# Eight experts on one core: all stores behind the last load, the first two x loads on one queue, b1 behind the first weights

## The chip, the core and the metric

The kernel runs on one core of a Trainium2 chip. The metric is the device time of one execution in microseconds, as the median of several executions. Data moves between the chip's memory (DRAM) and the core's on-chip memory over 16 DMA engines that all queues of the core share. A transfer is issued by a queue's owner: POOL (GpSimd), ACT (ScalarE) or SP (SyncE).

## The reference

Eight experts, each with 256 rows of width 512 and an inner width of 2048. All inputs and the output are float32.

```python
"x":  (8, 256, 512)    "w1": (8, 512, 2048)    "w2": (8, 2048, 512)
"b1": (8, 2048)        "b2": (8, 512)

h = np.matmul(x, w1) + b1[:, np.newaxis, :]
h = np.maximum(h, 0)
return (np.matmul(h, w2) + b2[:, np.newaxis, :]).astype(np.float32)
```

## The kernel before

**What one expert needs.** Its w1 and its w2 (4 MB each in float32) are loaded by POOL's queue, which casts to float16 on the way, so that 2 MB each land on chip. x of experts 2 to 7 takes the same way (0.25 MB landing each). `transposes(e)` turns x with eight small TensorE products and one VectorE copy into `xT`. `first_product(e)` runs 16 groups of four products (w1 against `xT`); ScalarE adds b1 and applies the maximum while it moves each group into `hT`. In the middle of it, after the ninth group, TensorE does `transposes(e + 1)`. `second_product(e)` puts b2 into two accumulators and adds 32 products of `hT` with w2; `store` then copies one accumulator with VectorE and the other with ScalarE into an `out` tile (0.5 MB) that goes to DRAM.

**Order.** The main loop runs over steps s from 0 to 10. Step s does `first_product(s)` (while s < 8) and then `second_product(s - 3)` (`LAG` is 3). TensorE's instructions and POOL's DMAs keep the order of the program. The DMAs of POOL's queue come from the list `ring`: each entry has the step from which it may be issued, and the list is worked off from its head, so an entry also waits for those ahead of it. w1 and w2 have three buffers each, so the load of w1 of expert 3 waits for the first product of expert 0, and so on; w2 of expert 7 has buffers of its own and comes in five pieces of 4, 4, 4, 2 and 2 rows out of 16.

**Stores.** `flush(e)` issues the store of expert e on POOL's queue. In the kernel before, experts 0, 1 and 2 have their `flush` in `ring` among the loads (step 4 on); experts 3 to 6 (`LATE`) have it behind all loads. The store of expert 5 is cut by rows (`PARTS`): 25 partitions go by SP as soon as the tile is ready, 96 and 7 by POOL. Expert 7 is stored in two halves by SP and ACT (L148, L149) as soon as each is copied.

**Start.** x of experts 0 and 1 comes as float32, one by SP and one by ACT, in pieces of 2 KB (L173), into a tile of its own (`x32`), and VectorE casts it (L186). b1 comes by ACT's queue behind x of expert 1 (L174). POOL issues w1 of expert 0, then b2 (L176), then makes two identity matrices, then enters the main loop. TensorE's program begins with 64 small products that turn b1 (L191); VectorE copies the result (L199); then come `transposes(0)` and the first product of expert 0. The turned b1 and the turned x share one accumulator buffer, so `transposes(0)` waits for that copy.

The main loop, with what fills `ring`, stands in full below.

Of the kernel before, what the change touches and what calls it, by code (L numbers as in the profile page):

```python
# [11 lines left out]
def kernel(  # L12
# [9 lines left out]
    nc = tc.nc  # L22
    fp32 = mybir.dt.float32
    fp16 = mybir.dt.float16
    E, T, H = x.shape
    M = w1.shape[2]
    P = 128
    nTB = T // P
    nKC = H // P
    nJ = M // P  # L30
    LAG = 3
    LATE = (3, 4, 5, 6)

# [1 line left out]
    nXF32 = 2  # L37

    def ordered(ins):
        return tc.keep_in_program_order(ins)  # L40

    singles = ctx.enter_context(tc.tile_pool(name="singles", bufs=1))
# [2 lines left out]
    w2t_pool = ctx.enter_context(tc.tile_pool(name="w2t", bufs=1))  # L45
    x_pool = ctx.enter_context(tc.tile_pool(name="xp", bufs=4))
    xT_pool = ctx.enter_context(tc.tile_pool(name="xTp", bufs=2))
    hT_pool = ctx.enter_context(tc.tile_pool(name="hT", bufs=LAG + 2))
    out_pool = ctx.enter_context(tc.tile_pool(name="outp", bufs=5))
    psum_x = ctx.enter_context(tc.tile_pool(name="psum_x", bufs=1, space=bass.MemoryType.PSUM))  # L50
    psum_h = ctx.enter_context(tc.tile_pool(name="psum_h", bufs=3, space=bass.MemoryType.PSUM))
    psum_o = ctx.enter_context(tc.tile_pool(name="psum_o", bufs=2, space=bass.MemoryType.PSUM))
# [5 lines left out]
    b1_rows = singles.tile([E * 2, M // 2], fp32)  # L58
    b1T = singles.tile([P, nJ, E], fp32)

    x16 = [None] * E
# [3 lines left out]
    hT = [None] * E  # L65
# [8 lines left out]
    def load_w1(e):  # L74
        w1_sb[e] = w1_pool.tile([P, nKC, M], fp16, tag="w1", name="w1sb")
        ordered(nc.gpsimd.dma_start(  # L76
            out=w1_sb[e], in_=w1[e].rearrange("(p kc) m -> p kc m", kc=nKC)
        ))

    def load_w2(e):  # L80
        src = w2[e].rearrange("(p j) h -> p j h", j=nJ)
        w2_sb[e] = []
        t = w2_pool.tile([P, nJ, H], fp16, tag="w2", name="w2sb")
        step = nJ if e < E - 2 else nJ // 2
        for lo in range(0, nJ, step):
            ordered(nc.gpsimd.dma_start(out=t[:, lo : lo + step, :], in_=src[:, lo : lo + step, :]))  # L86
            w2_sb[e].append((lo, lo + step, t[:, lo : lo + step, :]))
# [80 lines left out]
                    ))  # L168
        store(e, po)

    x32 = singles.tile([P, nXF32, nTB, H], fp32)
    for e in range(nXF32):
        (nc.sync if e == 0 else nc.scalar).dma_start(out=x32[:, e], max_dma_last_dim=2048, in_=x[e].rearrange("(p tb) h -> p tb h", tb=nTB))  # L173
    nc.scalar.dma_start(out=b1_rows, in_=b1.rearrange("e (s i) -> (e s) i", s=2))  # L174
    load_w1(0)
    ordered(nc.gpsimd.dma_start(  # L176
        out=b2_sb,
        in_=b2.rearrange("e h -> (e h)").rearrange("(o f) -> o f", o=1),
    ))
    make_identity(nc, ident)  # L180
    make_identity(nc, ident16)
    nc.vector.memset(ones1, 1.0)

    for e in range(nXF32):
        x16[e] = x_pool.tile([P, nTB, H], fp16, tag="x16", name="x16")
        nc.vector.tensor_copy(out=x16[e], in_=x32[:, e])  # L186

    pb = psum_x.tile([P, nJ, E, 2], fp32, tag="psx", name="pb")
    for j in range(nJ):
        for s in range(2):  # L190
            ordered(nc.tensor.matmul(  # L191
                out=pb[s * 64 : (s + 1) * 64, j, :, :],
# [5 lines left out]
    for s in range(2):  # L198
        nc.vector.tensor_copy(  # L199
            out=b1T[s * 64 : (s + 1) * 64, :, :], in_=pb[s * 64 : (s + 1) * 64, :, :, s]  # L200
# [5 lines left out]
    ring = []  # L206
    for s in range(1, E + LAG - 1):
        if s < E:
            if s >= nXF32:
                ring.append((s - 2, load_x, (s,)))  # L210
            ring.append((s - 2, load_w1, (s,)))
        if s >= LAG:
            ring.append((s - 2, load_w2, (s - LAG,)))
        if s >= 2 * LAG and s - 2 * LAG not in LATE:
            ring.append((s - 2, flush, (s - 2 * LAG,)))
    for lo, hi in ((0, 4), (4, 8), (8, 12), (12, 14), (14, 16)):
        ring.append((0, load_w2_piece, (E - 1, lo, hi)))
    for e in LATE:
        ring.append((e + LAG + 1, flush, (e,)))
# [40 lines left out]
```

## Time and profile before

| | |
|---|---|
| median of 6 runs | 183.0 us (182.57 to 183.25) |
| the profiled execution | 182.7 us, of which the span is 180.9 us |
| TensorE busy | 138.3 us, 76% of the span |
| ScalarE busy | 62.6 us, 35% |
| VectorE, GpSimd busy | 13.2 us, 20.3 us |
| moved by DMA, counted where it lands | 40.58 MB, mean 224 GB/s |
| the same, by POOL's queue (q0) alone | 38.71 MB in 4928 packets |
| read from DRAM, written to it | 71.39 MB, 4.19 MB |
| granted TensorE clock, mean | 0.924 of full speed |

The profile is one execution. Its span runs from the first to the last instruction; the execution's own time is 1.8 us longer, and the median of the runs stands 0.3 us above that. The shares of busy time are means over the whole span; a packet's time on a DMA engine can overlap with its neighbour's, so the DMA shares can add up to slightly over 100%. Times within the span are given in us from its start.

### The profile page before, as it was taken

The numbers are of one execution on the slowest core, as the hardware profiler recorded it, in microseconds if no ns is written. First come the engines' busy times: TensorE is split into PE (matmuls) and PEld (weight loads), VectorE is DVE, ScalarE is ACT, GpSimd is POOL, SyncE is SP. The second block draws the span as 40 slices with busy tenths as digits, with TensorE's granted clock in tenths as the row PEclk, the third lists the DMA queues.
The fourth block names the chain that finished last, engine by engine and source line by source line (L and its number), as shares of the span: only waits on it lengthen the run. The fifth ranks groups of instructions, "written<-read, shape, count | busy, mean of one in ns | idle before, by whom it ended". The sixth has DMA issues, their size and how long they took to land.

```text
span 180.9 us, 2129 instructions
## 1 busy us (share of the span) xinstructions
PE 138.3 (76%) x912; PEld 95.7 (53%) x912; DVE 13.2 (7%) x21; ACT 62.6 (35%) x137; POOL 20.3 (11%) x44
## 2 busy tenths in 40 slices
PE   0555989489650999939990899918999994999991
PEld 0544879469550754936480664907549641334340
DVE  0320011001000101010100101001010010010101
ACT  0022779538560340825080250722409601010101
POOL 7200030300300010211010100200004201112100
PEclk9999999969995589999999589996999999699999
DMA  5989998998999899899989998999998999999995
GB/s 186 288 178 234 232 214 192 205 255 181 230 232 221 185 232 232 189 216 232 228 185 221 236 225 185 228 257 207 232 221 190 284 232 249 211 215 217 212 375 229
DMA packets 5831, 40.58 MB, mean 224 GB/s; under 512 B 670, under 2 KB 686, under 8 KB 3774
## 3 DMA queue, kind: packets, MB, share of 16 engines
q0 software_dynamic: 4928, 38.71, 97.4%
q1 hardware_dynamic: 446, 0.89, 1.4%
q10 hardware_dynamic: 448, 0.85, 1.3%
q8 instruction: 7, 0.11, 0.2%
q14 instruction: 2, 0.02, 0.0%
HBM read 71.39 MB, written 4.19 MB: 418 GB/s over the span
## 4 chain that ended last, share of the span: by engine, by line
DMA 59%; PE 24%; issue 9%; another core or an unknown queue 4%; POOL 2%; ACT 0%; POOLq 0%; ACTq 0%
DMA x<-in_x_dram 25%; DMA w2sb<-in_w_dram 21%; PE po L162 16%; DMA w1sb<-in_w_dram 13%; PE ph L114 6%; PE po L156 1%; PE psx L101 1%; POOL w2sb L86 1%; POOL w1sb L76 1%; ACT out L140 0%; POOL out_dram L135 0%; POOL b_sb L176 0%; POOL ident masks.py:199 0%; POOL ident masks.py:197 0%
## 5 line engine op out<-in xcount | busy, mean ns | idle before, releaser
L114 PE MATMUL ph<-xT,w1sb 128*128 128x256 f16 x512 | 68.2, 299 | 9.2 <-DMA w1sb<-in_w_dram 9.2
L121 ACT ACTIVATE hT<-ph,b1T 128x256 f16<-128x256 f32 x128 | 57.0, 473 | 43.6 <-PE ph L114 43.3
L114 PEld LDWEIGHTS <-w1sb 128*128 128x128 f16 x512 | 61.5, 149 | 15.3 <-DMA w1sb<-in_w_dram 10.2
L162 PE MATMUL po<-w2sb,hT 128*128 128x512 f16 x224 | 51.2, 388 | 2.4 <-DMA w2sb<-in_w_dram 2.4
L162 PEld LDWEIGHTS <-hT 128*128 128x128 f16 x256 | 24.9, 100 | 35.3 <-issue 8.1
L140 ACT COPY out<-po 128x512 f32<-128x512 f32 x8 | 4.7, 590 | 60.4 <-PE po L162 60.4
L101 PE MATMUL psx<-ident,x 128*128 128x128 f16 x64 | 6.6, 265 | 20.4 <-DMA x<-in_x_dram 19.8
L101 PEld LDWEIGHTS <-x 128*128 128x128 f16 x64 | 5.3, 128 | 21.5 <-DMA x<-in_x_dram 20.7
L107 DVE COPY xT<-psx 128x1024 f16<-128x1024 f16 x8 | 5.5, 691 | 82.2 <-PE psx L101 82.2
L76 POOL DMA_DIRECT2D w1sb<-in_w_dram x8 | 4.5, 558 | 60.1 <-PE ph L114 59.3
L139 DVE COPY out<-po 128x512 f32<-128x512 f32 x8 | 5.5, 692 | 73.0 <-PE po L162 73.0
L86 POOL DMA_DIRECT2D w2sb<-in_w_dram x8 | 4.3, 536 | 48.6 <-PE po L162 48.6
L191 PE MATMUL pb<-ident,b_rows 16*64 16x16 f32 x64 | 3.7, 265 | 6.6 <-DMA b_rows<-in_b_dram 6.6
L191 PEld LDWEIGHTS pb<-ident,b_rows 16*64 16x64 f32 x64 | 3.6, 198 | 6.5 <-issue 6.5
L162 PE MATMUL po<-w,hT 128*128 128x512 f16 x32 | 7.1, 379 | 0.0
L135 POOL DMA_DIRECT2D out_dram<-out x8 | 4.3, 534 | 22.5 <-DMA w2sb<-in_w_dram 12.2
L121 ACT ACT_TABLE_LOAD x1 | 1.3, 1283 | 11.0 <-DVE b1T L199 11.0
L156 PE MATMUL po<-b_sb,ones 1*128 1x512 f16 x16 | 4.8, 379 | 0.0
L92 POOL DMA_DIRECT2D w<-in_w_dram x5 | 2.7, 538 | 14.3 <-DMA w2sb<-in_w_dram 13.5
L70 POOL DMA_DIRECT2D x<-in_x_dram x6 | 3.3, 551 | 4.8 <-DMA w2sb<-in_w_dram 4.2
L156 PEld LDWEIGHTS <-ones 1*128 1x128 f16 x16 | 0.9, 92 | 2.1 <-issue 2.1
L186 DVE CAST x<-x 128x1024 f16<-128x1024 f32 x2 | 1.4, 694 | 4.4 <-DMA x<-in_x_dram 4.3
(9 smaller groups left out, 2.6 us busy)
## 6 DMA issues: line engine op xcount, KB each, us to landing
w1sb<-in_w_dram POOLq DMA_DIRECT2D x8, 2048.0 KB, 33.6
w2sb<-in_w_dram POOLq DMA_DIRECT2D x6, 2048.0 KB, 45.3
out_dram<-out POOLq DMA_DIRECT2D x6, 512.0 KB, 29.7
w2sb<-in_w_dram POOLq DMA_DIRECT2D x2, 1024.0 KB, 25.4
x<-in_x_dram POOLq DMA_DIRECT2D x6, 256.0 KB, 38.9
w<-in_w_dram POOLq DMA_DIRECT2D x3, 512.0 KB, 29.5
x<-in_x_dram ACTq DMA_DIRECT2D x1, 512.0 KB, 5.3
x<-in_x_dram SPq DMA_DIRECT2D x1, 512.0 KB, 4.5
```

What stands on the lines that cost most here:

```text
L76: ordered(nc.gpsimd.dma_start(out=w1_sb[e], in_=w1[e].rearrange("(p kc) m -> p kc m", kc=nKC)))
L86: ordered(nc.gpsimd.dma_start(out=t[:, lo : lo + step, :], in_=src[:, lo : lo + step, :]))
L101: ordered(nc.tensor.transpose(out=pt[:, kc, tb * P : (tb + 1) * P], in_=x16[e][:, tb, :].rearrange("p (q kc) -> p q kc", kc=nKC)[:, :, kc] ...
L107: nc.vector.tensor_copy(out=xT[e], in_=pt)
L114: ordered(nc.tensor.matmul(out=ph, lhsT=w1_sb[e][:, kc, :].rearrange("p (q j) -> p q j", j=nJ)[:, :, j], rhs=xT[e][:, kc, :], start=(kc == 0),
L121: nc.scalar.activation(out=hT[e][:, j, :], in_=ph, func=mybir.ActivationFunctionType.Relu, bias=b1T[:, j, e : e + 1], scale=1.0,)
L135: ordered(nc.gpsimd.dma_start(out=dst[p0:p1], in_=src[p0:p1]))
L139: nc.vector.tensor_copy(out=out_sb[:, 0, :], in_=po[0])
L140: nc.scalar.copy(out=out_sb[:, 1, :], in_=po[1])
L156: ordered(nc.tensor.matmul(out=t, lhsT=ones1, rhs=b2_sb[0:1, e * H : (e + 1) * H], start=True, stop=False,))
L162: ordered(nc.tensor.matmul(out=po[tb], lhsT=hT[e][:, j, tb * P : (tb + 1) * P], rhs=t[:, j - lo, :], start=False, stop=(j == nJ - 1),))
L191: ordered(nc.tensor.matmul(out=pb[s * 64 : (s + 1) * 64, j, :, :], lhsT=b1_rows.rearrange("r (q j) -> r q j", j=nJ)[:, :, j], rhs=ident[0 ...
```

## The change

Five things change.

- `LATE` becomes all of experts 0 to 6: their stores are issued behind the last load. The `out` pool has eight buffers where it had five; `hT` has four where it had five.
- x of experts 0 and 1 goes by SP alone, in rows of 4 KB, into two buffers of the `out` pool in place of a tile of its own.
- b1 is loaded by POOL's queue, behind w1 of expert 0 and b2.
- w2 of expert 5 is loaded in two halves, as that of expert 6 was already.
- w2 of expert 7 comes in three pieces of 8, 4 and 4 rows.

```diff
-    LATE = (3, 4, 5, 6)
+    LATE = range(E - 1)
...
-    hT_pool = ctx.enter_context(tc.tile_pool(name="hT", bufs=LAG + 2))
-    out_pool = ctx.enter_context(tc.tile_pool(name="outp", bufs=5))
+    hT_pool = ctx.enter_context(tc.tile_pool(name="hT", bufs=LAG + 1))
+    out_pool = ctx.enter_context(tc.tile_pool(name="outp", bufs=E))
...
-        step = nJ if e < E - 2 else nJ // 2
+        step = nJ if e < E - 3 else nJ // 2
...
-    x32 = singles.tile([P, nXF32, nTB, H], fp32)
+    x32 = []
     for e in range(nXF32):
-        (nc.sync if e == 0 else nc.scalar).dma_start(out=x32[:, e], max_dma_last_dim=2048, in_=x[e].rearrange("(p tb) h -> p tb h", tb=nTB))
-    nc.scalar.dma_start(out=b1_rows, in_=b1.rearrange("e (s i) -> (e s) i", s=2))
+        x32.append(out_pool.tile([P, nTB, H], fp32, tag="out", name="x32"))
+        nc.sync.dma_start(out=x32[e], in_=x[e].rearrange("(p tb) h -> p tb h", tb=nTB))
     load_w1(0)
     ordered(nc.gpsimd.dma_start(
         out=b2_sb,
         in_=b2.rearrange("e h -> (e h)").rearrange("(o f) -> o f", o=1),
     ))
+    ordered(nc.gpsimd.dma_start(out=b1_rows, in_=b1.rearrange("e (s i) -> (e s) i", s=2)))
...
-        nc.vector.tensor_copy(out=x16[e], in_=x32[:, e])
+        nc.vector.tensor_copy(out=x16[e], in_=x32[e])
...
-        if s >= 2 * LAG and s - 2 * LAG not in LATE:
-            ring.append((s - 2, flush, (s - 2 * LAG,)))
-    for lo, hi in ((0, 4), (4, 8), (8, 12), (12, 14), (14, 16)):
+    for lo, hi in ((0, 8), (8, 12), (12, 16)):
         ring.append((0, load_w2_piece, (E - 1, lo, hi)))
     for e in LATE:
         ring.append((e + LAG + 1, flush, (e,)))
```

## The prediction

> **What bounds the kernel now.** I looked first for the resource that is never idle. On the page, the busy share of the 16 DMA engines over 40 slices and the split by queue say:
>
> ```profile
> DMA  5989998998999899899989998999998999999995
> ...
> q0 software_dynamic: 4928, 38.71, 97.4%
> q1 hardware_dynamic: 446, 0.89, 1.4%
> q10 hardware_dynamic: 448, 0.85, 1.3%
> ```
>
> From the second slice to the last but one nothing falls below 80%, and POOL's queue (q0) fills nearly all of it. The chain that ended last agrees: DMA holds 59% of it, TensorE 24%. So I ask of each edit what it adds to or takes from the work of the DMA engines, and only then what it does to TensorE.
>
> Next, the waits, for what TensorE and POOL lose:
>
> ```profile
> PE psx L101 <- DMA x<-in_x_dram: 19.8, 4, 6.7
> PE ph L114 <- DMA w1sb<-in_w_dram: 9.2, 4, 3.6
> PE pb L191 <- DMA b_rows<-in_b_dram: 6.6, 1, 6.6
> PE po L162 <- DMA w2sb<-in_w_dram: 2.4, 1, 2.4
> POOL x L70 <- DMA w2sb<-in_w_dram: 4.2, 1, 4.2
> ```
>
> TensorE waits for data. POOL's last row is another thing: x of expert 7 is POOL's 19th DMA, and it is issued when the 11th has landed; the other waits of this sort have the same distance, so at most eight of POOL's DMAs are under way.
>
> Then the timeline, for start and end:
>
> ```profile
> 1.27 0.49 ACTq L174 DMA_DIRECT2D b_rows<-in_b_dram  x1
> 6.56 3.71 PE L191 MATMUL pb<-ident,b_rows 16*64 16x16 f32 x64 [6.56 <-DMA b_rows<-in_b_dram]
> 12.04 0.69 DVE L107 COPY xT<-psx 128x1024 f16<-128x1024 f16 x1 [1.14 <-PE psx L101]
> 15.56 6.40 PE L114 MATMUL ph<-xT,w1sb 128*128 128x256 f16 x36 [3.55 <-DMA w1sb<-in_w_dram]
> 25.77 0.53 POOL L76 DMA_DIRECT2D w1sb<-in_w_dram  x1 [20.31 <-PE ph L114]
> ...
> 153.06 8.75 PE L162 MATMUL po<-w2sb,hT 128*128 128x512 f16 x32 [2.42 <-DMA w2sb<-in_w_dram]
> 169.82 7.08 PE L162 MATMUL po<-w,hT 128*128 128x512 f16 x32
> 170.32 0.55 POOL L135 DMA_DIRECT2D out_dram<-out  x1 [3.08 <-ACT out L140]
> 177.60 0.37 ACTq L149 DMA_DIRECT2D out_dram<-out  x1
> ```
>
> TensorE ends at 176.9, and expert 7's stores follow. The trace's packet records show the other racer: POOL's queue ends on the 16 engines between 176.7 and 178.25; expert 7's 16 packets per engine (2 KB, 84 to 88 ns each) run from 178.16 to 179.6. On the slowest engines the two join without a gap. TensorE's chain and the DMA work end together, so taking time from TensorE alone brings nothing.
>
> **Part by part.** The trace records when the last engine reports each transfer. Differences of neighbouring reports are what a transfer costs in a full queue: a whole w1 or w2 9.7 us, a half 4.79 and 4.87 (w2 of expert 6), a 4-row piece 2.50, 2.42, 2.46, a 2-row piece 1.24, 1.32, an x 1.24.
>
> *Stores of experts 0 to 2.* Among loads they cost 1.31, 1.31 and 1.27; those of experts 3 and 4, among stores, 1.26 and 1.24. Seven stores have to be moved either way, 3.6 MB of them by POOL. Moving three saves 3.89 - 3 x 1.25 = 0.1 at most; I take -0.1, bounds -0.15 and 0. The loads do come earlier: w2 of expert 5 (whole at 153.0) by two stores, 2.5; the last piece, now at 172.6, by three. What they gain is given back as stores behind them.
>
> *w2 of expert 7.* Now 166.44 - 163.94 for the first piece, then 2.42, 2.46, 1.24, 1.32: 9.94. After: 4.87 + 2 x 2.46 = 9.79, so -0.15.
>
> *w2 of expert 5 in halves.* Expert 6's halves cost 4.79 + 4.87 = 9.66; expert 5's whole cost 153.01 - 143.35 = 9.66. So 0, at worst +0.1. The Trainium skill ("DMA: Bandwidth & Descriptors", Anatomy of one DMA — SWDGE (gpsimd) path) fits a GpSimd DMA with a fixed 2.0 us plus its bytes; an estimate by it would put +2.0 on this split and -4.0 on the two pieces fewer. The halves above show no fixed part while the queue is full.
>
> *x of experts 0 and 1, and b1.* Now 32 packets of 2 KB per engine, then b1's one of 4 KB (159 to 180 ns), fill the engines from about 2.2 to 5.2, and w1 of expert 0 starts on each engine within a few ns of b1's end (5.13 to 5.44). After: 16 packets of 4 KB; the nearest row is b1's own, 0.16, so 16 x 0.16 = 2.6 against 32 x 0.084 = 2.7. Without b1 (0.16) w1 can start 0.3 earlier, if it is ready: POOL issued it at 1.26, and it cannot be told how long before 5.13 it was. b1 is paid behind it: +0.16. So between -0.15 and +0.16; I take 0, the middle, since neither end is nearer. SP issues both x in turn (0.43 each, so the second from 1.2); the first x's 8 packets per engine last until about 3.5, and the second is there by then.
>
> *b1 late.* It lands behind w1 of expert 0 and b2 (reports up to 15.68) at about 15.9 instead of 6.43. From its landing to the end of xT's copy, 6.56 to 12.73, are 6.2 us; so the first product starts at 22.1 instead of 15.56. That is 6.5 us off TensorE, and it is covered: the first product takes 9.9 (15.56 to 25.47, at partly half clock) or 7.7 (that of expert 1), so w1 of expert 3 is issued at 30.1 to 32.3 instead of 25.77. The queue has w1 of expert 2 and x of expert 3 until 36.7 on its fastest engine. From issue to first packet POOL needs at most 3.87 (w1 of expert 0, 1.26 to 5.13), so an issue up to 32.8 leaves no gap. Later loads have more: w1 of expert 4 follows at 38 to 40, its turn in the queue is at 57. TensorE catches up at the wait for x of expert 4 (6.75 idle before 59.02). The Trainium skill (same page, Latency and other measured facts) gives a first byte of 0.6 us to SP's and ACT's queues and 1 us to GpSimd's; an estimate by it would charge b1 only 0.4. The row charges the place in the queue.
>
> *Waits and buffers.* hT with four buffers: the one that step s writes was last read by the second product of s - 4, just ahead in TensorE's order; nothing. `out` with eight: x32's two slots come free at the casts (6.8). Eight DMAs under way: the store of expert 6 then waits for the last piece (about 169.9), is issued by 170.9, while the stores ahead fill the queue to 175; no gap.
>
> *TensorE's end.* x of expert 7 comes 1.25 earlier, w2 of expert 5's halves by 145.3 and 150.2, so the 2.4 us wait and the cold start behind it go: second products of experts 5 and 6 end at about 156 and 164, that of expert 7, held by its first piece (164.8), near 172. Its stores go out at 173 in place of 177.6 and mix with POOL's. What is late next is POOL's store queue: slowest engine 178.25 + 1.3 for expert 7's packets = 179.55, as now, and then the same 0.9 to 1.3 us to the span's end.
>
> The sum: -0.1 - 0.15 + 0 + 0 = -0.25, bounds -0.4 and +0.1. Where TensorE's chain was sometimes the later racer, its 5 us of slack add a little: I allow down to -0.6. Span 180.65, with the 1.8 around it 182.45; the median stood 0.3 above this profile's time: 182.7.
>
> **The rivals.** A difference of over 0.2% (0.37 us) is about what a measurement of this kernel can tell from no change.
>
> *Faster, by the tail.* If the median of now is set by TensorE's chain ending late in most runs (the profile's 182.7 is below the median 183.0) and w1 of expert 0 also starts 0.3 earlier, -0.8: 182.2. For it: the two racers are within 0.2 us. Against: the profiled run shows the slowest engines without a gap. That all of TensorE's 4.7 us is won is excluded by the seven stores behind the last load: 7 x 1.25 = 8.7 from 169.9.
>
> *Slower, by a dry queue.* The late b1 decides if w1 of expert 3 is issued after 32.8; each us beyond is a us lost. If the first product runs at half clock from end to end, 64 x 0.178 + 0.9 = 12.3, the issue comes at 34.7 and costs up to 1.9; with half of the 3.87 allowed for issue, nothing. I price it +0.9: 183.9. Against: the clock rose after 4.7 us of work in the run of before, and here b1's products lie just ahead.
>
> *Slower, by one engine.* The end is the slowest engine's. The trace shows seven instruction fetches of 0.9 us each, spread over six engines; if they fall on an engine that is last, +0.5: 183.5.
>
> *No move.* The order of the queue changes nothing at either end: 183.0.
>
> **How the numbers follow.** The forecast has 0.62; its spread of -0.6 to +0.1 puts 0.27 of that beyond -0.37, 0.33 within it, 0.02 above. Faster by the tail 0.15, dry queue 0.10, one engine 0.08, no move 0.05. Faster 0.27 + 0.15 = 0.42; same 0.33 + 0.05 = 0.38; slower 0.02 + 0.10 + 0.08 = 0.20. The range leaves out half of the dry queue and the far end of the tail: 181.9 to 183.5.
>
> **What would show it.** TensorE's first product begins near 22 and w1 of expert 3 is issued at 30 to 32, with the DMA share still at 9 in slices 7 to 9. The wait of L162 for w2sb is gone or under 1 us. The last piece lands near 170, TensorE ends near 172, and the last slices hold stores at about 375 GB/s (slice 39 of now). The forecast is wrong if the DMA share falls below 8 in any slice between, or if the stores behind the loads cost clearly more or less than 1.25 us each.

## The result, and the profile after

| | before | changed kernel |
|---|---|---|
| median | 182.88 us (39 runs, 182.54 to 183.42) | 183.64 us (17 runs, 183.43 to 184.48) |
| ratio | | 1.0048, 95% interval 1.0039 to 1.0057 |
| profiled execution | 182.7 us | 183.55 us |
| its span | 180.9 us | 181.8 us |

The change makes the kernel slower by 0.76 us, and the profiled span is longer by 0.87. Page, by slices and by queue:

```profile
DMA  5998999899999999999999999999998999999992
GB/s 213 249 231 189 231 231 216 179 239 231 211 195 231 231 206 198 209 253 202 202 231 231 202 202 231 202 220 213 231 231 182 218 209 224 207 230 214 398 401 109
...
q0 software_dynamic: 4816, 38.77, 96.8%
q1 hardware_dynamic: 462, 1.41, 2.1%
q10 hardware_dynamic: 144, 0.26, 0.4%
```

The DMA engines are as full as before, and slices 38 and 39, at 398 and 401 GB/s, are the stores behind the last load; but the last slice is at 2, where it was at 5: the engines have less to do just before the span ends. The waits of TensorE in the changed kernel:

```profile
PE psx L101 <- DMA x<-in_x_dram: 17.6, 4, 6.8
PE pb L192 <- DMA b_rows<-in_b_dram: 16.0, 1, 16.0
...
PE ph L114 <- DMA w1sb<-in_w_dram: 1.4, 1, 1.4
...
PE po L162 <- DMA w<-in_w_dram: 0.6, 1, 0.6
```

TensorE waits 16 us for b1 instead of 6.6, and only 1.4 and 0.6 us for w1 and w2 (9.2 and 2.4 before). The timeline at the start, and at the end:

```profile
15.99 3.71 PE L192 MATMUL pb<-ident,b_rows 16*64 16x16 f32 x64 [15.99 <-DMA b_rows<-in_b_dram]
...
22.21 5.88 PE L114 MATMUL ph<-xT,w1sb 128*128 128x256 f16 x36 [0.78 <-DVE xT L107]
...
31.91 0.53 POOL L76 DMA_DIRECT2D w1sb<-in_w_dram  x1 [25.69 <-PE ph L114]
```

```profile
164.47 7.07 PE L162 MATMUL po<-w,hT 128*128 128x512 f16 x32 [0.63 <-DMA w<-in_w_dram]
...
169.96 0.55 POOL L135 DMA_DIRECT2D out_dram<-out  x1 [2.27 <-DMA w<-in_w_dram]
...
171.44 0.36 SPq L148 DMA_DIRECT2D out_dram<-out  x1
...
172.19 0.38 ACTq L149 DMA_DIRECT2D out_dram<-out  x1
```

The first product starts at 22.21, w1 of expert 3 is issued at 31.91, TensorE ends at 171.5 in place of 176.9, and expert 7's two stores are issued 5.8 and 5.4 us earlier than before (177.60 for the one by ACT; the one by SP is the line below, from before). So far all is as forecast.

```profile
177.28 0.35 SPq L148 DMA_DIRECT2D out_dram<-out  x1
```

The end is not. The trace's reports of landing (last of 16 engines) say what came last:

| | before | changed kernel |
|---|---|---|
| last piece of w2 of expert 7 | 173.88 | 169.38 |
| POOL's last DMA, the store of expert 6 | 178.59 | 179.47 |
| SP's half of expert 7 | 179.35 | 178.11 |
| ACT's half of expert 7 | 179.99 | 179.64 |

The DMA engines finish 0.35 us earlier (179.64 against 179.99), and yet the span ends 0.87 later. What lies between can be read from the instructions of the program's end (line L255 in the kernel before, L254 in the changed one): a DRAIN on each engine (in the kernel before those of TensorE and VectorE end at 176.95 and 177.30, just behind their last work), and then a barrier that GpSimd collects. Each row gives shortest, median and longest duration in ns and the first and last start. First before, then the changed kernel:

```profile
L255 POOLq DRAIN  x3: 46/107/9813, 170.3 to 180.6; - x3
L255 SPq DRAIN  x3: 7/7/7, 180.1 to 180.4; - x3
```

```profile
L254 POOLq DRAIN  x3: 46/102/11053, 169.9 to 181.5; - x3
L254 SPq DRAIN  x3: 7/7/7, 179.8 to 181.2; - x3
```

POOL's first DRAIN starts as it issues its last DMA and is the longest of its row: 170.29 + 9.81 = 180.11 before, 169.94 + 11.05 = 180.99 now. SP's DRAIN, which follows when SP has seen every queue's reports, signals at 180.13 before and at 179.90 now. Before, the two came within 0.03 us of each other. Now SP is done 1.1 us before POOL. And POOL's drain ends 1.52 us after the last report of POOL's own DMAs in both: 180.11 - 178.59 and 180.99 - 179.47. From there to the span's end are 0.79 us in both.

Why POOL's queue ends later is seen in the times from issue to landing of the last store of POOL and of the two of expert 7 (512 and 256 KB each), before:

```profile
out_dram<-out POOLq DMA_DIRECT2D x1, 512.0 KB, 8.3
```

```profile
out_dram<-out SPq DMA_DIRECT2D x1, 256.0 KB, 2.1
out_dram<-out ACTq DMA_DIRECT2D x1, 256.0 KB, 2.4
```

and in the changed kernel:

```profile
out_dram<-out POOLq DMA_DIRECT2D x1, 512.0 KB, 9.5
```

```profile
out_dram<-out SPq DMA_DIRECT2D x1, 256.0 KB, 6.7
out_dram<-out ACTq DMA_DIRECT2D x1, 256.0 KB, 7.4
```

Issued early, the stores of SP and ACT mix with POOL's: they take 6.7 and 7.4 us in place of 2.1 and 2.4. The packet records show the order: their first packet starts at 175.42, 4.0 us after its issue, with 167 data packets of POOL (0.68 MB) still to start, and 255 of their 256 packets start before POOL's last data packet ends. Before, 19 did. POOL's last DMA takes 1.2 us more (9.5 against 8.3). Counted another way: the last piece of w2 lands 4.50 earlier, and three more stores behind it cost 3.8, so POOL's last report would have come at 177.9 if expert 7 had stayed behind it; it came 1.6 later. The 0.5 MB of expert 7 would be 1.25 at the price of the other stores; the rest is not accounted for.

### The profile page after: what moved, and what is told of

The parts are those of the page before. It is cut to its first block, busy times and chain, and to the rows that moved or that the text cites. A ratio compares the mean times of both kernels' runs of the same rounds, so it can differ in the third digit from the quotient of the medians.

```text
span 181.8 us, 2121 instructions
## 1 busy us (share of the span) xinstructions
PE 134.5 (74%) x912; PEld 94.2 (52%) x912; DVE 13.2 (7%) x21; ACT 62.5 (34%) x137; POOL 20.5 (11%) x44
## 4 chain that ended last, share of the span: by engine, by line
DMA 64%; PE 26%; POOL 2%; issue 1%; DVE 1%; ACT 0%; POOLq 0%
DMA x<-in_x_dram 40%; DMA w<-in_w_dram 16%; PE po L162 12%; PE ph L114 10%; DMA b_rows<-in_b_dram 7%; PE pb L192 2%; PE psx L101 2%; POOL w2sb L86 1%; POOL w1sb L76 1%; PE po L156 1%; DVE xT L107 0%; DVE b1T L200 0%; ACT out L140 0%; POOL b_sb L176 0%; POOLq L243 0%
## 5 line engine op out<-in xcount | busy, mean ns | idle before, releaser
L114 PE MATMUL ph<-xT,w1sb 128*128 128x256 f16 x512 | 66.8, 297 | 2.1 <-DMA w1sb<-in_w_dram 1.4
L121 ACT ACTIVATE hT<-ph,b1T 128x256 f16<-128x256 f32 x128 | 56.9, 473 | 32.3 <-PE ph L114 32.2
L162 PE MATMUL po<-w2sb,hT 128*128 128x512 f16 x224 | 49.6, 379 | 0.0
L162 PEld LDWEIGHTS <-hT 128*128 128x128 f16 x256 | 24.4, 98 | 32.4 <-issue 4.0
L101 PE MATMUL psx<-ident,x 128*128 128x128 f16 x64 | 5.8, 243 | 18.3 <-DMA x<-in_x_dram 17.6
L101 PEld LDWEIGHTS <-x 128*128 128x128 f16 x64 | 4.7, 122 | 19.4 <-DMA x<-in_x_dram 18.6
L86 POOL DMA_DIRECT2D w2sb<-in_w_dram x9 | 4.8, 535 | 53.7 <-PE po L162 53.7
L92 POOL DMA_DIRECT2D w<-in_w_dram x3 | 1.6, 557 | 0.0
## 6 DMA issues: line engine op xcount, KB each, us to landing
w<-in_w_dram POOLq DMA_DIRECT2D x2, 512.0 KB, 32.3
```

Of the source, the lines that this page charges most:

```text
L101: ordered(nc.tensor.transpose(out=pt[:, kc, tb * P : (tb + 1) * P], in_=x16[e][:, tb, :].rearrange("p (q kc) -> p q kc", kc=nKC)[:, :, kc] ...
L114: ordered(nc.tensor.matmul(out=ph, lhsT=w1_sb[e][:, kc, :].rearrange("p (q j) -> p q j", j=nJ)[:, :, j], rhs=xT[e][:, kc, :], start=(kc == 0),
L121: nc.scalar.activation(out=hT[e][:, j, :], in_=ph, func=mybir.ActivationFunctionType.Relu, bias=b1T[:, j, e : e + 1], scale=1.0,)
L162: ordered(nc.tensor.matmul(out=po[tb], lhsT=hT[e][:, j, tb * P : (tb + 1) * P], rhs=t[:, j - lo, :], start=False, stop=(j == nJ - 1),))
```

## The experiments

The theory that came from this, the tail theory, is written in the expectations below: the span ends 0.79 us after the later of two times, POOL's last report + 1.5, and the other queues' last report + 0.14. Its constants are from the two profiles above. Its rivals: the work theory (only the amount and order of DMA work count) and the late b1. The kernel before was timed again beside each group of runs, with medians from 182.78 to 182.91; the changed kernel was not, so differences from its 183.64 can be off by some 0.1 us.

**The disputed cost by itself.** The kernel before, with one line changed:

```diff
-            nc.scalar.dma_start(out=dst[:, 1, :], in_=out_sb[:, 1, :])
+            nc.gpsimd.dma_start(out=dst[:, 1, :], in_=out_sb[:, 1, :])
```

> The kernel before, with the second half of expert 7's store issued by POOL in place of ACT; the same bytes at the same point. Tail theory (the program cannot end before POOL's drain, and that ends 1.52 us after the last of POOL's DMAs has reported; 0.79 us later the span ends): POOL's last DMA is now reported near 180.2 instead of 178.59, so the drain ends near 181.7 and the span at 182.5, 1.6 us more than before: about 184.5. Work theory (only the DMA engines' work and its order count): the same packets by another queue, 0 to +0.3 us.

Measured: 184.44 us against 182.78, ratio 1.0088 (1.0069 to 1.0107).

```profile
L255 POOLq DRAIN  x3: 46/98/3901, 178.0 to 182.4; - x3
L255 SPq DRAIN  x3: 7/7/7, 180.8 to 182.2; - x3
```

POOL's last report is at 180.37, its drain ends at 178.02 + 3.90 = 181.93, 1.56 later; SP signals at 180.86 and then waits for it. The data landed only 0.4 later than in the kernel before, the span is 1.8 longer. The rest is the drain, and the work theory's 0.3 is out.

**Stores alone.** The kernel before with `LATE = range(E - 1)`, four buffers of hT and seven of out.

> The kernel before with the stores of experts 0 to 6 all behind the last load (hT four buffers, out seven) and nothing else of the change. Tail theory: TensorE ends near 172, expert 7's stores mix with POOL's, POOL's queue reports last near 179.5 to 179.8, the span is 181.8 to 182.1: the whole loss, +0.8 to +1.2 us on before. Theory of the late b1 or of x on one queue: those are not in this kernel, so 0 to -0.2 us.

Measured: 182.96 against 182.78, ratio 1.0015 (1.0000 to 1.0031). The tail theory's number, +0.8 to +1.2, was wrong, since I had taken TensorE's end from the whole change. With w2 of expert 5 in one piece TensorE still waits for it, 2.1 us, and its 32 products take 8.65 us, where those of expert 7 take 7.08:

```profile
150.05 8.65 PE L162 MATMUL po<-w2sb,hT 128*128 128x512 f16 x32 [2.09 <-DMA w2sb<-in_w_dram]
...
174.17 0.35 SPq L148 DMA_DIRECT2D out_dram<-out  x1
174.48 0.38 ACTq L149 DMA_DIRECT2D out_dram<-out  x1
```

Expert 7 is stored at 174.2 and 174.5, not at 171.4 and 172.2, and less of it goes ahead of POOL: 93 of its 256 packets start before POOL's last data packet ends, only 17 of them more than 1 us before. POOL's last report is at 178.25, the others' at 179.50, and the profiled span is 180.56 where the theory's rule gives 180.55 from these reports. In this profile late stores alone are not the loss; they have to meet an early end of TensorE. But the profiled execution, 182.32, has the lowest of the twelve times; four of them are 183.5 to 183.7, as long as the changed kernel, and no profile shows what happened there.

**b1 by ACT again**, all else of the change kept.

> The changed kernel with b1 on ACT's queue again, so that TensorE's first product starts near 15.5 instead of 22. Tail theory: nothing that sets the end moves, within 0.2 us of the changed kernel (183.6). Late-b1 theory: the loss comes back, 182.7 to 182.9.

Measured: 183.94, ratio to before 1.0062 (1.0046 to 1.0078). That is 0.3 above the changed kernel, a little more than the 0.2 allowed, and away from the 182.7 to 182.9 of the late b1. The late b1 is out: with b1 early, the loss is all there. POOL's last report is at 179.78, the drain's end at 181.26, the span 182.04.

**A step made later.** In the changed kernel, the copies of expert 7 are held until an earlier store has landed, by a write into that store's tile. The first try (`HELD` is 4, and `outs[e]` is the tile of expert e):

```diff
...
+        if e == E - 1:
+            nc.vector.memset(outs[HELD][:, 0, 0:1], 0.0)
+            nc.scalar.copy(out=outs[HELD][:, 1, 0:1], in_=b1T[:, 0, 0:1])
...
```

> The changed kernel, with the copies and so the stores of expert 7 held back until the store of expert 4 has landed (one more memset and one more copy, each of one column, write into that store's tile first). Nothing is made shorter and one step is made later. Tail theory: POOL's queue reports last near 178.3 (179.47 less 1.2 to 1.3 of packets that no longer go ahead), drain at 179.8; the other queues report last near 179.6 to 179.8; span 180.6 to 180.9, 1.0 us less than the changed kernel and about as before: 182.6 to 182.9. Work theory: a later store can only end later, 183.6 to 184.3.

Measured: 192.06, ratio 1.0496 (1.0469 to 1.0523). This says nothing on the order of the stores: the two held instructions were placed ahead of the copies of experts 5 and 6, and TensorE found no free accumulator. The waits show it, the two held instructions (L143, L144) and TensorE behind ScalarE's copy:

```profile
ACT out L144 <- DMA out_dram<-out: 28.5, 1, 28.5
...
DVE out L143 <- DMA out_dram<-out: 22.6, 1, 22.6
...
PE po L162 <- ACT out L146: 12.5, 1, 12.5
```

Expert 7's product ended at 186.1. The second try keeps all copies in program order.

> As the run before it (the changed kernel with the copies of expert 7 held until the store of expert 4 has landed), with the copies of all experts kept in program order, so that only expert 7 is held; in the run before, those of experts 5 and 6 stood behind the held one too and TensorE lost 13 us. Tail theory: POOL's queue reports last at 178.2 to 178.5, drain 1.52 later, the other queues last at 179.6 to 179.9, span 180.6 to 180.9: 1.0 us less than the changed kernel. Work theory: a later store ends later, 183.6 to 184.3.

Measured: 182.62, ratio to before 0.9992 (0.9977 to 1.0006), 1.0 us under the changed kernel.

```profile
175.86 0.06 DVE L142 MEMSET out<- 128x1 f32 x1 [13.51 <-DMA out_dram<-out]
175.86 0.69 DVE L144 COPY out<-po 128x512 f32<-128x512 f32 x1
...
176.52 0.38 ACTq L154 DMA_DIRECT2D out_dram<-out  x1
176.58 0.37 SPq L153 DMA_DIRECT2D out_dram<-out  x1
```

```profile
L259 POOLq DRAIN  x3: 46/98/9579, 170.0 to 180.2; - x3
L259 SPq DRAIN  x3: 7/7/7, 179.7 to 180.0; - x3
```

TensorE ends where it did, expert 7 is stored 5.1 and 4.3 us later, and the kernel is faster than the changed one. Now 39 of expert 7's 256 packets start before POOL's last data packet ends. POOL's last report is at 178.06, its drain ends at 169.99 + 9.58 = 179.57, SP signals at 179.71. The work theory, which could only lose from a later store, is out.

**POOL's queue relieved.** In the changed kernel POOL stores experts 0 to 3 alone; the others go, each whole, behind expert 7 on SP and ACT.

```diff
...
+    for e, eng in ((5, nc.sync), (6, nc.scalar), (4, nc.sync)):
+        dst, src = pending.pop(e)
+        ordered(eng.dma_start(out=dst, in_=src))
```

> The changed kernel with the stores of experts 4, 5 and 6 taken from POOL's queue: 5 and then 4 by SP, 6 by ACT, each whole and behind that queue's half of expert 7. POOL then has the stores of experts 0 to 3 alone. Tail theory: POOL's queue reports last before 178, its drain is over before 179.5, and SP's and ACT's last packets set the end: reported 179.4 to 179.9, span 180.3 to 180.9, about 1.1 us less than the changed kernel and 0 to 0.5 less than before. Work theory: the same bytes, no change, 183.6.

Measured: 182.76, ratio 0.9991 (0.9979 to 1.0003), with the narrowest spread of the kernels with twelve runs (182.67 to 183.01).

```profile
L257 POOLq DRAIN  x3: 109/190/20505, 155.3 to 180.5; - x3
L257 SPq DRAIN  x3: 7/7/7, 179.6 to 179.9; - x3
```

POOL's drain ends at 155.26 + 20.51 = 175.77, long before SP's signal at 179.61. The gain over the changed kernel is 0.9 instead of 1.1: the span, 180.90, is 0.56 longer than the rule gives. GpSimd's last DRAIN, which in the other kernels starts 0.17 us after the barrier's clearing of semaphores and takes 46 ns, starts 0.54 after it here and takes 190 ns (the median of the row above). The run with the cut by rows below shows the same. Why, stays open. It is not POOL's idle time alone: in the first try of the hold POOL's drain was over 5.0 us before SP's signal, and the closing steps took their usual 0.77. The records show one more difference: the last instruction fetch of 8 KB starts at 181.17 and 181.44 in these two profiles, after the span's end, and 6 us or more before the barrier in the eleven others. Nothing here shows that it is the cause.

**Early stores in the changed kernel.** `LATE = (3, 4, 5, 6)` and the `flush` of experts 0 to 2 in `ring` again.

> The changed kernel with the stores of experts 0 to 2 among the loads again, all else of the change kept. Tail theory: the last piece lands 3.8 us later, TensorE ends near 175.4, expert 7's stores come later and go ahead of few of POOL's packets; POOL's queue reports last at 178.4 to 178.9, span 180.7 to 181.2: 182.6 to 183.0. If the loss lies in b1, in x or in the pieces: 183.6 as the changed kernel.

Measured: 183.10, ratio 1.0010 (0.9999 to 1.0021). Undoing this one part takes back 0.5 of the 0.76. TensorE ends near 176.6 again, later than the 175.4 forecast, and the median is 0.1 above the forecast's 183.0, for POOL's queue is later too: last report 179.18, the others' 180.47, a tie as in the kernel before, both 0.5 to 0.6 later than there.

**w2 of expert 5 in one transfer**, all else of the change kept.

> The changed kernel with w2 of expert 5 in one transfer again, all else kept. The second product of expert 5 then waits until the whole has landed (150) in place of the first half (145). Tail theory: TensorE ends 2 to 2.5 us later, near 173.8; expert 7's stores are issued at 174 to 174.7 and get behind most of POOL's packets; POOL's queue reports last at 178.2 to 178.8, span 180.5 to 181.1: 0.7 to 1.2 us less than the changed kernel, though TensorE is later. Work theory: 0 to -0.1 us, and if TensorE's end counts, +2.

Measured: 183.17, ratio 1.0008 (0.9991 to 1.0026), runs from 182.15 to 183.81. The sign is the tail theory's, the step is not: expert 7 is stored only 0.4 later (171.83 and 172.59), since its own first piece held it in the changed kernel as well. In the profiled execution (183.13) POOL's last report is at 179.09, the span 181.35, within 0.04 of the rule. Why two of the twelve runs are as low as 182.15 and 182.40 was not settled.

**The rows of expert 5 cut as in the changed kernel**, added to the relieved POOL.

> The changed kernel with the stores of experts 4, 5 and 6 behind expert 7 on SP and ACT, as in the run in which POOL kept those of 0 to 3 alone, but with expert 5 cut by rows as in the changed kernel: 25 partitions by SP early, 96 and 7 late. In that earlier run the 16 engines' last reports on the last queue lay 1.4 us apart (178.03 to 179.41). Tail theory: POOL's drain is over by 177; the end is the slowest engine's, which has two rows of 4 KB less, 0.3 us: last report 179.0 to 179.2, span 180.4 to 180.7, 182.3 to 182.6. If the cut by rows does nothing for the slowest engine: 182.76 as that run.

Measured: 182.81, ratio 1.0001 (0.9990 to 1.0013); last report 179.40 as without the cut. It does nothing for the last report, where 0.2 to 0.4 less was forecast.

**The start alone**, in the kernel before: both x by SP in 4 KB, b1 by POOL.

> The kernel before with the start of the change alone: x of experts 0 and 1 by SP in rows of 4 KB, b1 by POOL's queue behind b2. Tail theory: POOL's last report and TensorE's end both come as much earlier as the DMA queue starts earlier, 0 to 0.4 us: 182.5 to 182.9. If the late b1 or the single queue costs something at the end: over 183.1.

Measured: 183.04, ratio 1.0015 (1.0001 to 1.0029): no gain, above the forecast's 182.9. w1 of expert 6 does land 0.2 earlier (109.74 against 109.95), but w2 of expert 3 behind it lands 0.5 later; see below.

**A shorter hold**, behind expert 2's store.

> The changed kernel with the copies of expert 7 held until the store of expert 2 has landed (about 173.2), so that its stores are issued near 174 in place of 171.4 and 172.2; held behind expert 4 they were issued at 176.5 and the time was 182.62. Tail theory: an amount between, since fewer packets go ahead of POOL's: POOL's queue reports last at 178.3 to 179.0, span 180.6 to 181.3: 182.7 to 183.3. Work theory: the changed kernel's 183.6 or more.

Measured: 182.42, ratio to before 0.9981 (0.9967 to 0.9994).

```profile
173.27 0.69 DVE L144 COPY out<-po 128x512 f32<-128x512 f32 x1
...
173.93 0.38 ACTq L154 DMA_DIRECT2D out_dram<-out  x1
173.99 0.37 SPq L153 DMA_DIRECT2D out_dram<-out  x1
```

```profile
L259 POOLq DRAIN  x3: 46/103/9851, 169.9 to 180.2; - x3
L259 SPq DRAIN  x3: 7/7/7, 179.6 to 180.0; - x3
```

This version beats both kernels, by 0.19% (0.06 to 0.33) the one before and by 1.2 us the changed one. The forecast, an amount between the longer hold and no hold (182.7 to 183.3), was wrong: the shorter hold is no worse than the longer one, and their intervals overlap. The gain on the kernel before is the best of eleven edits and barely clear of noise; the gain on the changed one is not in doubt. Issued at 174, 129 of expert 7's 256 packets start before POOL's last data packet ends, but only 19 of them more than 1 us before, so that POOL is hardly held up (its last report 178.20, drain end 179.72; the others 179.49, SP's signal 179.68). And the DMA engines stay full, at a share of 1.00 from 176 to 177 and 0.95 from 177 to 178, against 0.88 and 0.84 with the longer hold: again both ends meet.

The rule against the profiles (last reports and spans in us):

| kernel | POOL + 1.51 | others + 0.14 | later + 0.79 | span |
|---|---|---|---|---|
| before | 180.10 | 180.13 | 180.92 | 180.90 |
| changed | 180.98 | 179.78 | 181.77 | 181.77 |
| half of 7 by POOL | 181.88 | 179.70 | 182.67 | 182.70 |
| stores alone | 179.76 | 179.64 | 180.55 | 180.56 |
| b1 by ACT | 181.29 | 179.59 | 182.08 | 182.04 |
| hold behind 4, first try | 184.00 | 189.02 | 189.81 | 189.79 |
| hold behind 4, in order | 179.57 | 179.65 | 180.44 | 180.48 |
| early stores | 180.69 | 180.61 | 181.48 | 181.48 |
| w2 of 5 whole | 180.60 | 179.61 | 181.39 | 181.35 |
| start alone | 180.56 | 180.61 | 181.40 | 181.39 |
| hold behind 2 | 179.71 | 179.63 | 180.50 | 180.50 |

The two kernels with POOL relieved are the exceptions: 180.34 and 180.33 by the rule, 180.90 and 180.89 measured. Each row is one execution. For the stores alone and for the hold behind 4, in order, it has the lowest of twelve times, so the rule is not tested on their longer ones.

## Why the prediction was wrong

**The step that failed** is the last of "TensorE's end": "slowest engine 178.25 + 1.3 for expert 7's packets = 179.55, as now, and then the same 0.9 to 1.3 us to the span's end." The first half was right: all packets were reported by 179.64, 0.35 earlier than before. The second half took the way from the last packet to the end as one number for all queues. It is 0.93 us for SP and ACT and 2.3 for POOL. Before, POOL's queue ended 1.4 us ahead of the others and its drain was hidden to 0.02 us; the page does not list DRAIN among the costs, and I had not followed the instructions of the program's end. I wrote that expert 7's stores "mix with POOL's" and did not ask which queue would then be last. Of the signs that I had named for a wrong forecast one came, at the very end: POOL's last store, that of expert 6, reports 1.78 us behind the one ahead of it, where it was 1.09 before.

**The sum of -0.25** was of the right size for what it was a sum of: -0.35. But it came near partly by luck, since two errors offset each other. The loads ended 4.50 earlier (169.38 against 173.88), of which three stores are 3.89: 0.61 saved, where I had 0.15 from the pieces of w2. Behind the loads the last report took 10.26 in place of 6.11, 4.15 more for three stores that I priced at 3.75. The term for the stores was mis-sized on both sides: I took 3.89 against 3 x 1.25, and so -0.1. The runs show a cost that is not in the stores' own rows: w2 of expert 3, the load just ahead of the first early store, takes 10.01 us on the first engine to report in the kernel before, 9.94 in that with half of expert 7 by POOL, 10.35 with the start alone and 10.48 with early stores in the changed kernel, against 9.65 to 9.75 in the nine kernels whose stores all come behind the loads. So early stores cost 0.3 to 0.8 more than I gave them.

**b1 late** was right: 22.1 forecast, 22.21 measured; w1 of expert 3 issued at 31.91, inside 30.1 to 32.3; no slice of the DMA row between start and end fell below 8; with b1 early the time was not better. The slower rival by a dry queue did not happen. Nor did the one by one engine: of the store of expert 4, which lands as the mixing begins, the first and last engines report 1.42 us apart, 1.53 before. So the slower side had 0.20 of the chances for mechanisms that were not the cause.

**TensorE's chain**: forecast to end near 172, measured 171.5; the wait for w2 under 1 us (0.6); the first five stores behind the loads 1.26 each (169.38 to 175.68). In one place I named 172.6 as the last piece's landing; that was the fourth piece, the last came at 173.9, and the 169.9 that I built on was worked from the right one.

**x and b1 at the start**, taken at 0: the queue started 0.2 to 0.3 earlier in the trace, but as an edit alone it brought nothing (1.0015), so 0 stands, with the reason open.

**The two rules of the Trainium skill** ("DMA: Bandwidth & Descriptors"): the fixed 2.0 us per DMA (Anatomy of one DMA — SWDGE (gpsimd) path) again does not show in a full queue, where expert 5's halves came 4.85 and 4.87 us apart on the first engine; the first byte's 0.4 us between the queues (Latency and other measured facts) is no measure of b1's delay, which was 9.4 us, for its place in the queue.

**The range** ended at 183.5, 0.14 short of the median. It took in a slowest engine (+0.5) but no cost behind the last landing.

## What to carry to other kernels

At a kernel's end, ask not only when the last byte lands but which queue it came by: the reports of each queue, the DRAIN of each engine and the barrier behind them are the last links of the chain, and a tie there is invisible on a page of busy shares. Work that is taken off one racer can come back as a new order of the other: here an engine that finished 5 us earlier sent its stores into the DMA engines ahead of the queue that was last. And where two queues share the DMA engines, try to put last the transfer whose queue closes more cheaply, if need be by holding it: here 0.93 us from the last report to the end for SP and ACT, 2.30 for POOL.

## What the runs showed that I had not expected

POOL's drain at the end of the program lasted until 1.48 to 1.56 us after the last report of POOL's DMAs in eleven profiles (1.35 and 1.36 in the two where that report came at 174.3 and 174.4), with a last DMA of 512 KB as with one of 256 KB. SP's signal came 0.14 to 0.26 us after the last report where that was SP's or ACT's.

With stores among the loads, the load ahead of the first of them took 0.3 to 0.8 us longer; the stores themselves cost 1.2 to 1.3 there, hardly more than behind the loads, and the loads ahead of the later ones were not longer. What in the store does this was not tried.

In the two kernels with POOL relieved, GpSimd's own closing steps took 0.5 us longer, by a cause that stays open; against the kernel before, that ate all that relieving POOL's queue should have gained (180.34 by the rule, 180.90 measured, 180.90 before).
